# RMS norms of an encoder trunk: sums and factors by 32x32 block turns instead of row products

## The chip, the cores and the metric

The kernel runs on one core of a Trainium2 chip. A core has TensorE (PE in the profile: matrix products, with its weight loads listed apart as PEld), VectorE (DVE), ScalarE (ACT), GpSimd (POOL) and SyncE (SP, which here only issues transfers). PE writes to PSUM, which the kernel divides into eight banks of 128 x 512 float32; the other data live in SBUF, 128 partitions wide. The metric is the device time of one execution in microseconds (us); the figure for a kernel is the median of its runs.

## The reference

Two layers of a bidirectional encoder trunk over 512 tokens of width 1024, all float32:

```python
h = rms_norm(x, attn_norm_g[l])
proj = h @ w_in[l]      # latents, rotary key, GQA q/k/v, pool channels, 3 gates
... three branches: latent attention, grouped-query attention, pooling
merged = gates[0]*(o_mla @ w_b0) + gates[1]*(o_gqa @ w_b1) + gates[2]*(o_pool @ w_b2)
x = x + merged @ w_out[l]
hf = rms_norm(x, ffn_norm_g[l])
u = depthwise_conv(hf @ ffn_w_up[l], ...)          # 2 x 2816 columns, width 3
x = x + (silu(u_gate) * u_val) @ ffn_w_down[l]

def rms_norm(x, g):
    return x * rsqrt(mean(x*x, axis=-1) + 1e-6) * g
```

There are thus four norms over the 1024 features: one ahead of attention and one ahead of the feed-forward part, in each of two layers. Smaller norms (latents, heads) exist too; of those the change touches one step of the grouped-query heads' norm.

## The kernel before, in words

The residual stream lies in SBUF feature-major: `XM` is eight chunks (kc) of 128 features (partitions) by 512 tokens. Every product is made of three products of 32-bit "fp32r" operands, each number split into a high and a low half: `HH` and `HL` are the halves of x times the gain g (without the token's factor), `wh` and `wl` those of a piece of the weights. Weights stream in by SP; ACT makes `wh`, and POOL (or DVE) makes `wl = raw - wh`, three pieces ahead of use (`LA = 3`). A block of output is 8 chunks x 3 products = 24 products of 128x512. So the token's factor rsqrt(mean + eps) is not needed before a product; it is multiplied in when a PSUM bank is emptied. It is needed in two layouts:

- by token on partitions (`rt`, used through `rtok(b)` for the four blocks b of 128 tokens), for results that come token-major: the latents, GQA q, k and v;
- by token along the free axis, the same on all partitions (`rbc`, 128 x 512), for results that come feature-major: pool channels, gates, the up-projection.

A norm runs so. As each chunk of x is finished, ACT squares it and POOL (DVE in the first norm) adds the squares into `sq`, 128 x 512, element by element, so `sq` still has 128 partial sums for each token, one on each partition. `norm_finish` then takes the sums over partitions: four float32 products with two columns of ones, one for each block of 128 tokens, into the one bank "S". DVE makes mean plus eps, POOL raises it to the power -0.5 (128 x 8), which is `rt`. For the other layout DVE splits `rt` into halves `rth` and `rtl` and multiplies each into the identity (`dgh`, `dgl`, 128 x 512); `norm_rows` multiplies ones with these two diagonals on PE and ACT copies the result to `rbc`.

What sets the order of the work: each engine executes its own queue in order. The queues are written by a planner inside the program, the class `Clock`: every instruction is booked with an estimated cost on its engine, `chain` issues the next step of a sequence when the step before is finished by these books, `need` moves the planner's time on until a key is done, and `has` asks whether a key is done by now. So the place of an instruction in its queue follows from booked costs; on the chip it then waits on semaphores for its data. PE products advance the planner's time.

The places that matter here:

- `layer(l, ...)`: first the latent projection, token-major, into the banks acc, acc, ST, ST (`tok_major(latb, 384)`); then four pooling groups, feature-major, into AV, AV, mi, S (`feat_major`, which yields after each of the eight chunks); then GQA q (`gqb`), k and v.
- The latents are emptied by ACT with the factor (`lat_evac`), then normalized; the chain waits for `rt`. The tables of rotary factors are made on POOL after `rt`, too, in the first layer.
- Norm of the first layer's attention: `norm_finish` is called after the sixth chunk of the first pooling group, `norm_rows` after the second group. Second layer: `norm_finish` right after the latent projection, `norm_rows` after the first group.
- Feed-forward norms: `norm_finish` after the first block of 24 products of the up-projection, `norm_rows` after the second. The up-projection has 44 blocks of 24 products, in three tags of two banks each.
- `gq_mean`: DVE turns the sums of squares of the 8 heads x 4 blocks (`ssr`, 128 x 32) into mean plus eps, one tensor_scalar; Newton steps on DVE follow. Around it in DVE's queue stand the steps that empty the pooling product's banks (`opl`), which later gate products need.
- The start: DVE fills a few constants, PE runs nine idle products of ones (`idle`), SP loads x, the first weights, then the constants `C`.

Of the kernel before, what the change touches and what calls it, by code (L numbers as in the profile page):

```python
# [10 lines left out]
F32 = mybir.dt.float32  # L11
F32R = mybir.dt.float32r
# [6 lines left out]
P = 128  # L19
T = 512  # L20
# [35 lines left out]
PRM_MQ = PRM_B + 2 * FC  # L56
NPRM = PRM_MQ + 2

C_ID, C_CG, C_SG, C_CM, C_SM, C_EDGE = 0, 128, 384, 640, 768, 896
NCST = C_EDGE + 64  # L60


def _order(br):
# [59 lines left out]
class Clock:  # L123
# [129 lines left out]
def trunk(ctx: ExitStack, tc: tile.TileContext, x, w, prm, gb, cst, out):  # L253
# [48 lines left out]
    def f(ap):  # L302
        return ap.bitcast(F32)
# [55 lines left out]
    def mm(o, lhsT, rhs, start, stop):  # L359
        PE.matmul(o, lhsT=lhsT, rhs=rhs, start=start, stop=stop)  # L360
        ck.to(ck.now + max(0.107, rhs.shape[-1] / 2370.0))
# [15 lines left out]
    idr = cp.tile([P, P], F32R, tag="idr", name="idr")  # L377
# [3 lines left out]
    mhalf = cp.tile([P, 1], F32, tag="mhalf", name="mhalf")  # L381

    unit = cp.tile([P, P], F32R, tag="unit", name="unit")

# [68 lines left out]
            return [guess, *[lambda to=to: newton(to) for to in (y, y, a)], lambda: done(*key)]  # L453
        return [go, lambda: done(*key)]

    def norm_finish(gen, sq, out):

        need(*[("sq", gen, kc) for kc in range(KC)])
        s2 = ps("S")
        for b in range(4):  # L460
            mm(s2[:, 2 * b:2 * b + 2], sq[:, b * P:b * P + P], f(ones[:, :2]), True, True)
        rt = out["rt"] = small("rt", [P, 8])
        rh, rl = small("rth", [P, 8], F32R), small("rtl", [P, 8], F32R)
        dg = out["dg"] = slot("dgh", F32R), slot("dgl", F32R)

        def mean():
            V.tensor_scalar(rt, s2[:, :8], 1.0 / D, EPS, ALU.mult, ALU.add)
            free("S")

        def diag(n):  # L470
            r = f((rh, rl)[n]).rearrange("p (b t) -> p b t", t=2)[:, :, 0:1]
            V.tensor_tensor(dg[n][:, :T].rearrange("p (b q) -> p b q", b=4), bc(ident[:, None, :], [P, 4, P]),
                            bc(r, [P, 4, P]), ALU.mult)

        chain(mean, *rsqrt_steps(rt, 8, ("rt", gen)), lambda: V.tensor_copy(rh, rt),
              lambda: V.tensor_tensor(rl, rt, f(rh), ALU.subtract), lambda: diag(0), lambda: diag(1),
              lambda: done("dg", gen), after=0.4)

    def norm_rows(gen, out, tag):

        need(("dg", gen))
        r = ps(tag)
        for n in range(2):
            mm(r, ones, out["dg"][n][:, :T], n == 0, n == 1)
        rbc = out["rbc"] = slot("rbc")
        chain(lambda: (A.activation(rbc[:, :T], r, AF.Copy), free(tag), done("rbc", gen)))

    def copy(out, in_, psum=True, bias=C_BIAS):

        n = 1  # L490
        for d in out.shape[1:]:
            n *= d
        act = max(ck.now, ck.free.get("ACT", 0.0)) + 0.09 + 0.00084 * n
        dve = max(ck.now, ck.free.get("DVE", 0.0)) + 0.07 + (0.00105 if psum else 0.00053) * n
        if dve + bias < act:
            V.tensor_copy(out, in_, psum)
        else:
            A.activation(out, in_, AF.Copy)

    def bc(ap, shape):  # L500
        return ap.to_broadcast(shape)
# [26 lines left out]
    def layer(l, sq, xsrc):  # L528
# [68 lines left out]
        nrm = {}  # L597
        ltags = ("acc", "acc", "ST", "ST")
        latb = [ps(t) for t in ltags]
        tok_major(latb, 384)  # L600
        if l:
            norm_finish(G1, sq, nrm)

        def rtok(b):
            return nrm["rt"][:, 2 * b:2 * b + 1]

        mx = [slot("mx") for _ in range(4)]
        ssc = small("ssc", [P, 4, 2])
# [23 lines left out]
        if l:  # L632
            latents()


        mixed = {}
# [44 lines left out]
        for g in range(4):  # L681
            acc = ps(ptags[g])
            for n, _ in enumerate(feat_major(acc, G1)):
                if l == 0 and g == 0 and n == 5:
                    norm_finish(G1, sq, nrm)
                    latents()
# [74 lines left out]
            chain(add, lambda: done("gqr", l, b), after=ck.fin - ck.now)  # L761

        def gq_mean():
            V.tensor_scalar(ssr[:, 0:32], ssr[:, 0:32], 1.0 / 64, EPS, ALU.mult, ALU.add)

        def gq_token():
            s_ = ssr[:, 0:32].rearrange("p (b h) -> p b h", b=4)
            V.tensor_tensor(s_, s_, bc(nrm["rt"].rearrange("p (b t) -> p b t", t=2)[:, :, 0:1], [P, 4, 8]), ALU.mult)

        def gq_norm(b):  # L770
            o = gqo[b][:, :T].rearrange("p (h f) -> p h f", f=64)
# [712 lines left out]
            chain(*steps)  # L1484

        n = 0
        for c in range(FC):
            for part in range(2):
                tag = tags[n % 3]
                n += 1  # L1490
                acc = ps(tag)
                run(feat_major(acc, G2))
                if n == 1:
                    norm_finish(G2, sq, fin)
                if n == 2:
                    norm_rows(G2, fin, "mi")
                up_evac(c, part, acc, tag)

        last = l == L - 1
# [49 lines left out]
    sq = slot("sq")  # L1549
    nc.scalar.dma_start(prms[0][:, :PRM_W0], prm[0][:, :PRM_W0])  # L1550
    warm = small("warm", [P, 1], bufs=1)
    V.memset(mhalf, -0.5)
    V.memset(warm, 0.0)
    A.activation(warm, warm, AF.Exp)
    V.memset(f(ones), 1.0)
    G.memset(f(unit), 0.0)
    G.memset(f(unit[:, 0:1]), 1.0)
    idle = ps("mi")
    for _ in range(9):
        PE.matmul(idle, lhsT=ones, rhs=ones[:, None, :].to_broadcast([P, 4, P]), start=True, stop=True)  # L1560
    free("mi")
    for kc in range(KC):
# [125 lines left out]
def _constants():  # L1688
    cg, sg = _tables(64)
    cm, sm = _tables(32)  # L1690
    t = np.arange(T)
    edge = []
    for w in WINDOWS:
        cnt = np.clip(t + w - w // 2, 0, T) - np.clip(t - w // 2, 0, T)
        r = w / cnt
        edge += [r[:8], r[-8:]]
    edge = np.broadcast_to(np.concatenate(edge).astype(np.float32), (P, 64))
    return np.concatenate([np.eye(P, dtype=np.float32), cg, sg, cm, sm, edge], axis=1)


# [22 lines left out]
```

## Time and profile before

| | us |
|---|---|
| median of 3 runs | 1612.09 (1611.22 to 1614.61) |
| the profiled execution's own time | 1611.31 |
| its span, first to last instruction | 1609.5 |
| PE busy | 1600.2 |
| POOL busy | 1002.6 |
| DVE busy | 950.0 |
| ACT busy | 793.8 |

The profile is of one execution. Its page gives the busy time of each engine, the span in 40 slices, the queues of transfers, the chain of work that ended last, and groups of instructions. Further views of the same trace are used: the waits (who waited for whom), groups by line or by tile (count, then least, median and most ns), and the timeline (start in us, length in us, engine, line, operation, out<-in, shape, count; a bracket gives the idle time just before it and what ended it). Most instructions are issued by small helpers, so L360 is any product, L221 any tensor_tensor, L233 any tensor_scalar, L225 any scalar_tensor_tensor; the tile names tell them apart. Lengths of PE's products overlap: what one costs is the distance between starts.

### The profile page before, as it was taken

To read this page: it belongs to the slowest core of one execution; us is meant where nothing else is said; L and a number is where in the kernel's file an instruction comes from. 1 tells how busy PE (TensorE), PEld (TensorE's weight loads), DVE (VectorE), ACT (ScalarE), POOL (GpSimd) and SP (SyncE) were. 2 spreads that over 40 slices of the span, in tenths; PEclk is the share of its full clock that TensorE was granted. 3 is DMA by queue.
4 is the path that set the end of the run, shared out by engine and by line. 5 is a ranking of instruction groups with operands and counts; after the bars stand their busy time and mean duration, and the time that the engine had idled before them with its cause. 6 is when DMAs were issued, how large, how long until landed. Compare 5 with 4: busy or idle time off the path is not lost.

```text
span 1609.5 us, 20515 instructions
## 1 busy us (share of the span) xinstructions
PE 1600.2 (99%) x7131; PEld 1313.1 (82%) x7131; DVE 950.0 (59%) x1533; ACT 793.8 (49%) x1430; POOL 1002.6 (62%) x889
## 2 busy tenths in 40 slices
PE   9999999999999999999999999999999999999999
PEld 8888888788888888888888888888888888888888
DVE  6878867765276666611047788678552766666000
ACT  6457757663444444433244577576533444444221
POOL 3864985854666665654568549868547566665542
PEclk9999999999999999999999999999999999999999
DMA  5432234414323323233335222343242222222331
GB/s 198 130 104 67 76 115 114 117 59 145 104 87 97 92 92 94 93 115 111 105 105 131 92 76 70 104 139 96 79 144 92 92 92 92 93 93 103 118 112 46
DMA packets 85928, 164.37 MB, mean 102 GB/s; under 512 B 25024, under 2 KB 47040, under 8 KB 85824
## 3 DMA queue, kind: packets, MB, share of 16 engines
q1 hardware_dynamic: 80928, 162.85, 32.5%
q8 instruction: 56, 0.92, 0.2%
q10 hardware_dynamic: 4896, 0.21, 0.2%
q14 instruction: 48, 0.39, 0.1%
HBM read 149.33 MB, written 13.63 MB: 101 GB/s over the span
## 4 chain that ended last, share of the span: by engine, by line
PE 93%; DVE 2%; issue 1%; POOL 1%; ACT 1%; DMA 1%; SPq 0%; ACTq 0%; POOLq 0%
PE ps_acc L360 41%; PE ps_AV L360 22%; PE ps_ST L360 22%; PE ps_S L360 3%; PE ps_mi L360 3%; DVE XM L221 1%; DMA tf<-dtq 1%; POOL wl L221 0%; DVE mgl L221 0%; DVE gt L225 0%; ACT mgh L214 0%; DMA qa<-nm 0%; DMA dtq<-tr 0%; PE ps_mi L1560 0%; POOL gqr L221 0%
## 5 line engine op out<-in xcount | busy, mean ns | idle before, releaser
L221 POOL TENSOR_TENSOR wl<-raw,wh 128x512 fp32r<-128x512 f32 (+2 forms) x502 | 659.9, 1325 | 464.8 <-ACT wh L214 377.5
L214 ACT ACTIVATE wh<-raw 128x512 fp32r<-128x512 f32 (+1 forms) x521 | 308.3, 607 | 124.0 <-PE ps_ST L360 40.7
L225 DVE SCALAR_TENSOR_TENSOR a<-u,prm,a 128x512 f32<-128x512 f32 x176 | 239.0, 1359 | 79.4 <-ACT a L214 74.1
L360 PE MATMUL ps_acc<-HH,wh 128*128 128x512 f32 x592 | 234.9, 397 | 0.5 <-DVE gt L221 0.5
L360 PE MATMUL ps_acc<-HL,wh 128*128 128x512 f32 x592 | 234.1, 395 | 0.0
L360 PE MATMUL ps_acc<-HH,wl 128*128 128x512 f32 x592 | 233.4, 394 | 0.0
L360 PEld LDWEIGHTS ps_acc<-HH,wl 128*128 128x128 f32 x592 | 111.2, 188 | 27.3
L360 PEld LDWEIGHTS ps_acc<-HH,wh 128*128 128x128 f32 x592 | 111.5, 188 | 26.1 <-issue 1.1
L360 PEld LDWEIGHTS ps_acc<-HL,wh 128*128 128x128 f32 x592 | 111.3, 188 | 25.4
L360 PE MATMUL ps_AV<-HH,wh 128*128 128x512 f32 x288 | 114.3, 397 | 1.6 <-DVE y L233 1.6
L360 PE MATMUL ps_AV<-HL,wh 128*128 128x512 f32 x288 | 113.8, 395 | 0.0
L360 PE MATMUL ps_AV<-HH,wl 128*128 128x512 f32 x288 | 113.5, 394 | 0.0
L229 DVE TENSOR_REDUCE nm<-ps_S 128x1 fp32r<-128x512 f32 x128 | 87.6, 685 | 39.9 <-PE ps_S L360 38.3
L221 POOL TENSOR_TENSOR al<-a,ah 128x512 fp32r<-128x512 f32 x44 | 58.1, 1320 | 84.9 <-ACT ah L214 56.5
L360 PE MATMUL ps_ST<-HH,wh 128*128 128x512 f32 x240 | 95.3, 397 | 0.0
L360 PE MATMUL ps_ST<-HL,wh 128*128 128x512 f32 x240 | 95.0, 396 | 0.0
L360 PE MATMUL ps_ST<-HH,wl 128*128 128x512 f32 x240 | 94.3, 393 | 0.0
L214 ACT ACTIVATE a<-u,prm 128x512 f32<-128x512 f32 x88 | 71.8, 816 | 33.3 <-DVE u L221 33.3
L214 ACT ACTIVATE ah<-a 128x512 fp32r<-128x512 f32 x44 | 27.8, 631 | 116.1 <-DVE u L249 110.7
L214 ACT ACTIVATE a<-a 128x512 f32<-128x512 f32 x44 | 27.8, 632 | 113.0 <-DVE u L249 113.0
L214 ACT ACTIVATE HH<-XM,prm 128x512 fp32r<-128x512 f32 x32 | 23.1, 722 | 106.2 <-DVE XM L221 55.1
L214 ACT ACTIVATE ps_ST<-ps_ST 128x512 f32<-128x512 f32 x86 | 49.9, 581 | 41.3 <-PE ps_ST L360 38.9
(385 smaller groups left out, 3751.0 us busy)
## 6 DMA issues: line engine op xcount, KB each, us to landing
raw<-w SPq DMA_DIRECT2D x228, 512.0 KB, 3.5
raw<-w SPq DMA_DIRECT2D x13, 384.0 KB, 3.1
XM<-x SPq DMA_DIRECT2D x16, 256.0 KB, 3.9
dtq<-tr SPq DMA_DIRECT2D x16, 192.0 KB, 3.3
dtk<-tr SPq DMA_DIRECT2D x16, 192.0 KB, 4.2
tf<-dtq SPq DMA_DIRECT2D x48, 64.0 KB, 2.5
tf<-dtk SPq DMA_DIRECT2D x48, 64.0 KB, 2.7
raw<-w SPq DMA_DIRECT2D x6, 448.0 KB, 3.4
```

Of the source, the lines that this page charges most:

```text
L214: return self.eng.activation(out, in_, func, **k)
L221: return self.eng.tensor_tensor(out, *a)
L225: return self.eng.scalar_tensor_tensor(out, *a)
L229: return self.eng.tensor_reduce(out, in_, *a, **k)
L360: PE.matmul(o, lhsT=lhsT, rhs=rhs, start=start, stop=stop)
```

## The change

Each norm's sums go another way. `norm_begin`, called at the start of the stage, turns `sq` on DVE in 32x32 blocks as soon as the last square is added; a sum over groups of 32 elements then leaves `part`, 128 x 16: for each of the 16 groups of 32 tokens, the sums over each quarter of the partitions, tokens now on partitions within each quarter. `norm_finish` multiplies this on PE with one constant 128 x 128 matrix `C_GRP`, which adds the four quarters and puts the result on all of them. DVE makes mean plus eps, POOL the power, now on 128 x 16. From these 16 columns both layouts come on DVE: `tokens` picks the column of the partition's quarter with the constant `C_SEL` and adds over four, giving `rt` (128 x 4); `rows` turns the 16 columns, each repeated 32 times, in 32x32 blocks, giving `rbc`. `norm_rows`, the diagonals, the halves and ACT's copy are gone. `norm_finish` is now called after every chunk of the pooling groups and of the up-projection's blocks; it issues the product when the planner's books have `part` ready, or at a forced place. `latents()` is set up before the pooling groups in both layers.

The other edits: `gq_mean` becomes a scalar_tensor_tensor with a broadcast tile of eps; the tile `idr` and its copy go; at the start `ones` is filled first, there are eight idle products instead of nine, and the constants are 1104 columns wide instead of 960.

```diff
-    def norm_finish(gen, sq, out):
-        need(*[("sq", gen, kc) for kc in range(KC)])
+    def norm_begin(gen, sq):
+        t, part = slot("sqT"), small("prt", [P, 16])
+        parts[gen] = part
+        chain(([("sq", gen, kc) for kc in range(KC)], lambda: V.transpose(t[:, :T], sq[:, :T])),
+              lambda: V.tensor_reduce(part, t[:, :T].rearrange("p (j r) -> p j r", r=32), AX.X, ALU.add),
+              lambda: done("prt", gen), after=0.0)
+
+    def norm_finish(gen, out, force=False):
+        if gen not in parts or not (force or ck.has(("prt", gen))):
+            return
+        need(("prt", gen))
         s2 = ps("S")
-        for b in range(4):
-            mm(s2[:, 2 * b:2 * b + 2], sq[:, b * P:b * P + P], f(ones[:, :2]), True, True)
...
+        mm(s2[:, :16], C[:, C_GRP:C_GRP + P], parts.pop(gen), True, True)
+        a, a4 = small("fac", [P, 16]), small("fac4", [P, 16])
+        rt, rbc = out["rt"], out["rbc"] = small("rt", [P, 4]), slot("rbc")
         def mean():
-            V.tensor_scalar(rt, s2[:, :8], 1.0 / D, EPS, ALU.mult, ALU.add)
+            V.tensor_scalar(a, s2[:, :16], 1.0 / D, EPS, ALU.mult, ALU.add)
             free("S")
...
-        chain(mean, *rsqrt_steps(rt, 8, ("rt", gen)), lambda: V.tensor_copy(rh, rt),
-              lambda: V.tensor_tensor(rl, rt, f(rh), ALU.subtract), lambda: diag(0), lambda: diag(1),
-              lambda: done("dg", gen), after=0.4)
-
-    def norm_rows(gen, out, tag):
...
+        def tokens():
+            V.tensor_tensor(a4, a, C[:, C_SEL:C_SEL + 16], ALU.mult)
+            V.tensor_reduce(rt, a4.rearrange("p (b g) -> p b g", g=4), AX.X, ALU.add)
+            done("rt", gen)
+        def rows():
+            V.transpose(rbc[:, :T].rearrange("p (j r) -> p j r", r=32), bc(a.unsqueeze(2), [P, 16, 32]))
+            done("rbc", gen)
+        chain(mean, lambda: G.tensor_tensor(a, a, bc(mhalf, [P, 16]), ALU.pow), tokens, rows, after=0.3)
...
+        norm_begin(G1, sq)
         tok_major(latb, 384)
-        if l:
-            norm_finish(G1, sq, nrm)
...
             for n, _ in enumerate(feat_major(acc, G1)):
-                if l == 0 and g == 0 and n == 5:
-                    norm_finish(G1, sq, nrm)
-                    latents()
-            if g == (l == 0):
-                norm_rows(G1, nrm, "acc")
+                norm_finish(G1, nrm, g == 1 and n == 6)
...
-            V.tensor_scalar(ssr[:, 0:32], ssr[:, 0:32], 1.0 / 64, EPS, ALU.mult, ALU.add)
+            V.scalar_tensor_tensor(ssr[:, 0:32], ssr[:, 0:32], 1.0 / 64, bc(eps, [P, 32]), ALU.mult, ALU.add)
...
+        norm_begin(G2, sq)
...
-                run(feat_major(acc, G2))
-                if n == 1:
-                    norm_finish(G2, sq, fin)
-                if n == 2:
-                    norm_rows(G2, fin, "mi")
+                for i, _ in enumerate(feat_major(acc, G2)):
+                    norm_finish(G2, fin, n == 3 and i == 6)
...
-    V.memset(mhalf, -0.5)
+    V.memset(f(ones), 1.0)
     V.memset(warm, 0.0)
     A.activation(warm, warm, AF.Exp)
-    V.memset(f(ones), 1.0)
+    V.memset(mhalf, -0.5)
+    V.memset(eps, EPS)
...
-    for _ in range(9):
+    for _ in range(8):
...
-    at(30.0, lambda: V.tensor_copy(idr, ident))
```

More of the change, by code (lines that the diff above doesn't have):

```diff
@@ L57 @@
 NPRM = PRM_MQ + 2
-C_ID, C_CG, C_SG, C_CM, C_SM, C_EDGE = 0, 128, 384, 640, 768, 896
-NCST = C_EDGE + 64
+C_ID, C_CG, C_SG, C_CM, C_SM, C_EDGE, C_GRP, C_SEL = 0, 128, 384, 640, 768, 896, 960, 1088
+NCST = C_SEL + 16
 def _order(br):
@@ L376, in trunk @@
     C = cp.tile([P, NCST], F32, tag="C", name="C")
-    idr = cp.tile([P, P], F32R, tag="idr", name="idr")
     xsp = dp.tile([KC, P, T], F32, tag="xsp", name="xsp")
@@ L381, in trunk @@
     mhalf = cp.tile([P, 1], F32, tag="mhalf", name="mhalf")
+    eps = cp.tile([P, 1], F32, tag="eps", name="eps")
     unit = cp.tile([P, P], F32R, tag="unit", name="unit")
@@ L454, in rsqrt_steps @@
         return [go, lambda: done(*key)]
-    def norm_finish(gen, sq, out):
-        need(*[("sq", gen, kc) for kc in range(KC)])
-        s2 = ps("S")
-        for b in range(4):
-            mm(s2[:, 2 * b:2 * b + 2], sq[:, b * P:b * P + P], f(ones[:, :2]), True, True)
-        rt = out["rt"] = small("rt", [P, 8])
-        rh, rl = small("rth", [P, 8], F32R), small("rtl", [P, 8], F32R)
-        dg = out["dg"] = slot("dgh", F32R), slot("dgl", F32R)
+    def norm_begin(gen, sq):
[4 more added lines that the diff above has]
+              lambda: done("prt", gen), after=0.0)
@@ L479, in norm_rows @@
-    def norm_rows(gen, out, tag):
[L481 to L486, printed above, removed]
+        def tokens():
+            V.tensor_tensor(a4, a, C[:, C_SEL:C_SEL + 16], ALU.mult)
+            V.tensor_reduce(rt, a4.rearrange("p (b g) -> p b g", g=4), AX.X, ALU.add)
+            done("rt", gen)
@@ L498, in copy @@
             A.activation(out, in_, AF.Copy)
+    parts = {}
     def bc(ap, shape):
@@ L630, in latents @@
                   *rsqrt_steps(ssc.rearrange("p a b -> p (a b)"), 8, ("ssc", l)), lat_norm)
-        if l:
-            latents()
+        latents()
         mixed = {}
@@ L1697, in _constants @@
     edge = np.broadcast_to(np.concatenate(edge).astype(np.float32), (P, 64))
-    return np.concatenate([np.eye(P, dtype=np.float32), cg, sg, cm, sm, edge], axis=1)
+    p = np.arange(P)
+    group = (p[:, None] % 32 == p[None, :] % 32).astype(np.float32)
+    sel = (p[:, None] // 32 == np.arange(16)[None, :] % 4).astype(np.float32)
+    return np.concatenate([np.eye(P, dtype=np.float32), cg, sg, cm, sm, edge, group, sel], axis=1)
 def kernel(**inputs):
```

9 lines of the change are left out of this document (2 added, 7 removed).

## The prediction

> **What bounds the kernel now.** I read the page first: part 1 (busy time of each engine), the slices, and part 4 (the chain that ended last).
>
> ```profile
> PE 1600.2 (99%) x7131; PEld 1313.1 (82%) x7131; DVE 950.0 (59%) x1533; ACT 793.8 (49%) x1430; POOL 1002.6 (62%) x889
> PEclk9999999999999999999999999999999999999999
> PE 93%; DVE 2%; issue 1%; POOL 1%; ACT 1%; DMA 1%; SPq 0%; ACTq 0%; POOLq 0%
> ```
>
> TensorE (PE) works nearly without a break, at full granted clock in every slice, and 93% of the chain is PE. So a product that disappears from PE shortens the run by its own spacing, a stall of PE that disappears by its length, and work on other engines counts only where PE ends up waiting for it. The view of waits, PE alone, gives the stalls (us in total, times, longest):
>
> ```profile
> PE ps_AV L360 <- DVE y L233: 1.6, 1, 1.6
> PE ps_mi L1560 <- DVE ones L249: 1.1, 1, 1.1
> PE ps_mi L360 <- DMA qa<-nm: 0.7, 1, 0.7
> ```
>
> Beside the 1.1 us before PE's first instruction and the 1.6 us stall, nothing is above 0.7 us.
>
> **Term 1, products removed.** The timeline of PE around the second layer's feed-forward norm:
>
> ```profile
> 1241.07 0.40 PE L360 MATMUL ps_acc<-HH,wl 128*128 128x512 f32 x1
> 1241.31 0.95 PE L360 MATMUL ps_S<-ones,sq 128*128 128x2 f32 x8
> 1242.12 0.48 PE L360 MATMUL ps_ST<-HH,wh 128*128 128x512 f32 x1
> 1242.43 0.39 PE L360 MATMUL ps_ST<-HL,wh 128*128 128x512 f32 x1
> 1242.66 0.40 PE L360 MATMUL ps_ST<-HH,wl 128*128 128x512 f32 x1
> ...
> 1247.57 0.39 PE L360 MATMUL ps_ST<-HH,wl 128*128 128x512 f32 x1
> 1247.80 0.39 PE L360 MATMUL ps_mi<-dgh,ones 128*128 128x512 f32 x1
> 1248.02 0.46 PE L360 MATMUL ps_mi<-dgl,ones 128*128 128x512 f32 x1
> 1248.32 0.42 PE L360 MATMUL ps_AV<-HH,wh 128*128 128x512 f32 x1
> ```
>
> Ordinary products start 0.23 us apart (1242.43 to 1242.66); the 0.4 us beside each is its length in a pipeline, not its price. From 1241.07 to 1242.43 would be two steps, 0.46; it is 1.36. So the four float32 sums, eight records, cost 0.90 us. From 1247.57 to 1248.32 would be one step; it is 0.75, so the two row products cost 0.52. A norm pays 1.42, and there are four (the groups of these tiles, all with counts over the run; columns after the colon are least, median and most ns):
>
> ```profile
> L360 PE MATMUL ps_S<-ones,sq x32: 166/251/251, 26.4 to 1242.0; 128*128 128x2 f32 x32
> L360 PE MATMUL ps_acc<-dgh,ones x2: 392/395/398, 34.3 to 828.7; 128*128 128x512 f32 x2
> L360 PE MATMUL ps_mi<-dgh,ones x2: 389/393/397, 447.5 to 1247.8; 128*128 128x512 f32 x2
> ```
>
> The two row products of each attention norm I count at the plain spacing, 0.46. Sum: 4 x 0.90 + 2 x 0.52 + 2 x 0.46 = 5.6 us; taken **-5.6**.
>
> **Term 2, the product added.** One float32 product of a 128x128 constant with 16 columns at each norm. The nearest row is the one just used: four such products with 2 columns cost 0.90, so 0.23 for one, in two records. Fourteen more columns at 0.23 us per 512 columns are 0.01. From below: half of it, 0.11, if the neighbours hide the weight loads; from above 0.46, one record more at each end. I take 0.25: **+1.0** (0.4 to 1.8).
>
> **Term 3, what the product waits for.** The partial sums need a turn of sq and a sum over 32 elements on DVE, behind the last addition. Rows of the first norm (timeline) and the two durations (groups):
>
> ```profile
> 20.72 4.95 DVE L221 TENSOR_TENSOR sq<-sq,sqt 128x512 f32<-128x512 f32 x4
> 26.43 0.95 PE L360 MATMUL ps_S<-ones,sq 128*128 128x2 f32 x8
> 27.41 0.17 DVE L233 TENSOR_SCALAR rt<-ps_S 128x8 f32<-128x8 f32 x1 [1.75 <-PE ps_S L360]
> L245 DVE STREAM_TRANSPOSE osum<-oinv 128x512 f32<-128x512 f32 x16 | 11.3, 708 | 1.8 <-POOL oraw L221 0.9 <-ACT oinv L214 0.2
> L229 DVE TENSOR_REDUCE ssr<-gqs 128x8 f32<-128x512 f32 x8 | 5.2, 673 | 0.0
> ```
>
> Sums end at 25.67; turn 0.71 and sum 0.67 end at 27.05, and DVE is free for them (idle 1.75). PE reaches the place at 26.43 if the product goes where the four go now, after the sixth step of the first pooling group: it waits about 0.6. Does it go there? The code issues it at the first step at which the planner's own clock (a count of booked costs, no time of the chip) has the sums ready. The books add 0.61 + 0.13 + 0.61 + 0.15 for turn and sum to a last addition at 23.2, giving 24.7, and reach the sixth step at 24.8: same place, by a hair. One step later the wait is gone (0.7 us a step); one earlier it is 1.3. **+0.6** (0 to 1.3).
>
> The feed-forward norms have no such wait: there the planner, which until now stops at the sums, goes on and issues the product some four steps (2.8 us) into the second column block. The four sums at 1241.31 already had the finished additions, so turn and sum, 1.4 us, end by 1242.7; PE gets there near 1244. In the second layer's attention norm the product follows the whole latent projection, near 823, and this is its last addition:
>
> ```profile
> 809.20 1.29 POOL L221 TENSOR_TENSOR sq<-sq,sqt 128x512 f32<-128x512 f32 x1
> ```
>
> Both cost nothing.
>
> **Term 4, the other edit.** The mean of the squares, 128x32, and what stood around it (DVE, POOL and PE timelines; second layer first, then the first layer's same step):
>
> ```profile
> 876.72 8.30 DVE L233 TENSOR_SCALAR ssr<-ssr 128x32 f32<-128x32 f32 x1
> 884.94 0.74 DVE L225 SCALAR_TENSOR_TENSOR opl<-ps_AV,prm,oph 128x512 fp32r<-128x512 f32 x1
> 879.19 5.79 POOL L221 TENSOR_TENSOR wl<-raw,wh 128x288 fp32r<-128x288 f32 x5
> 883.98 0.29 PE L360 MATMUL ps_ST<-wh,HL 128*128 128x288 f32 x1
> 885.82 0.47 PE L360 MATMUL ps_AV<-HH,wh 128*128 128x512 f32 x1 [1.56 <-DVE y L233]
> ...
> 76.66 0.22 DVE L233 TENSOR_SCALAR ssr<-ssr 128x32 f32<-128x32 f32 x1
> 80.18 1.21 DVE L225 SCALAR_TENSOR_TENSOR y<-yt,y 128x32 f32<-128x32 f32 x1
> ```
>
> The same instruction took 0.22 once and 8.30 once, ending when POOL's unbroken run (to 884.98) ended. Queued behind it is opl, which empties the bank that PE's first gate product needs: PE starts at 885.82 instead of about 884.1. The new form is a SCALAR_TENSOR_TENSOR of the same size; small ones with POOL running take up to 1.21, one POOL instruction. Then opl is done by 879 and the stall goes. Next late is the second gate bank, needed 24 steps or 5.6 us after the first; the first layer has that order and no ps_AV stall. **-1.7** (0 to -1.7).
>
> A rule of the Trainium skill speaks against this. SBUF — State Buffer, "Who interferes with whom", says that a DVE instruction with two SBUF inputs also contends with a GpSimd one that reads SBUF, and that the lock is held for a whole instruction. By that rule the new form (eps is a second SBUF input) stays exposed, and the sum would be -4.1 instead of -5.8. The 8.30 fits no lock for one POOL instruction, so the trace goes beyond the rule; the 1.21 row agrees with it.
>
> **Term 5, the start.** One of nine idle products goes and ones is filled first.
>
> ```profile
> 1.11 4.21 PE L1560 MATMUL ps_mi<-ones 128*128 128x512 f32 x9 [1.11 <-DVE ones L249]
> 3.71 0.72 ACT L214 ACTIVATE HH<-XM,prm 128x512 fp32r<-128x512 f32 x1 [1.03 <-DMA prm<-prm]
> 4.69 0.76 PEld L360 LDWEIGHTS ps_acc<-wh,HH 128*128 128x128 f32 x2
> ```
>
> The first real load at 4.69 waits for HH (done 4.43), so little is won: **-0.1** (-0.4 to +0.3). The constants grow by 15%; first used near 27 us, they are covered. The copy idr on DVE goes, unseen by PE.
>
> **What moves off PE's path, at nothing.** DVE loses a cast, a subtraction and two 128x512 products, and gains a turn, two sums, a small product and the final turn; ACT loses the copy of rbc. POOL's power takes 16 columns for 8:
>
> ```profile
> L221 POOL TENSOR_TENSOR rt<-rt,mhalf x4: 1644/1652/1654, 27.7 to 1242.5; 128x8 f32<-128x8 f32 x4
> 40.61 2.59 POOL L221 TENSOR_TENSOR wl<-raw,wh 128x512 fp32r<-128x512 f32 x2
> 46.00 0.40 PE L360 MATMUL ps_AV<-wh,HH 128*128 128x512 f32 x1
> 450.96 3.05 POOL L221 TENSOR_TENSOR wl<-raw,wh 128x512 fp32r<-128x512 f32 x2 [4.59 <-PE ps_AV L360]
> 832.10 1.68 POOL L221 TENSOR_TENSOR wl<-raw,wh 128x512 fp32r<-128x512 f32 x1 [2.37 <-issue]
> 840.51 5.60 PE ps_S L360 x24
> ```
>
> It lies between 1.65 and 3.3. Behind it on POOL stand weight halves (wl); behind the factor on ACT stand the latent evacuations or the convolution steps, and behind those the other halves (wh). With the two tiny DVE sums (0.17 to 1.2 each) the factor comes 0.6 to 3.7 us later in the attention norms. The cover: the first wl of the pair at 40.61 ends at 41.9 and is used at 46.0, 4.1 us; the one that starts at 450.96 ends near 452.4 and is used in the fourth column block near 456.4, 4.0 us. In the second layer's attention norm the half ready at 833.8 is used at 840.5, 6.7 us. So late by 3.7 still costs nothing; beyond 4 us PE pays one for one. The rows of the factor themselves come earlier in the first layer (no row products to await).
>
> **Sum.** -5.6 + 1.0 + 0.6 - 1.7 - 0.1 = -5.8 us. The profiled execution took 1611.31 (span 1609.5), giving 1605.5; it lies 0.8 below the median 1612.09. Against the median I forecast **1606.3**.
>
> **Rivals.** *The DVE stall stays* (small steps of either form stuck behind POOL): term 4 is nothing, 1608.0. For: 128x32 steps that wait for POOL at all; against: the SCALAR_TENSOR_TENSOR row above, also beside POOL's run, took 1.21. *New stalls take the gain:* the planner's order shifts by under a microsecond at each norm, and waits like the 0.7 us one multiply in attention; with 3 to 6 us of them, 1609 to 1612. Against: both layers' attention now has under 2 us of stalls. *Slower:* a tiny DVE step of the new factor is held as long as the mean was, 8.3 us, at every norm. It decides from 4 us on: PE then pays 8.3 - 4.1 in the first layer, 8.3 - 4.0 in both feed-forwards, and some 1.6 in the second attention norm (cover 6.7), 14.4 in all: 1620.7. Against: the step of the TENSOR_SCALAR form among them reads PSUM and took 0.17 at all four norms.
>
> **Chances.** Forecast 0.55 (own range 1604.8 to 1608.2); stall stays 0.2; new stalls 0.15; slower 0.07; better still by the remaining small stalls 0.03. About 0.2%, 3.2 us, is what a measurement here can tell from no change: faster is below 1608.9. All but little of the first two cases and the last lies there, 0.70 with a part taken off for unseen shifts; within 0.21; slower 0.09. The range for 8 in 10, out to most of the new-stall case: 1604.3 to 1611.3.
>
> **What would show it.** Right: two ps_S records from the constant at each norm, no row products; a PE wait of about 0.6 at 27 us; no 8.3 us mean at 877 and no ps_AV stall at 885; feed-forward blocks back to back. Wrong: PE waiting for wl or wh within 20 us behind a norm (POOL's power or a held tiny step), a new long DVE step beside POOL's run, or PE waits in attention above 2 us together.

## The result, and the profile after

| | before | after |
|---|---|---|
| median, us | 1611.22 (1609.09 to 1614.61, 5 runs) | 1590.24 (1589.31 to 1593.7, 5 runs) |
| the profiled execution | 1611.31 | 1593.7 |
| its span | 1609.5 | 1591.8 |

The ratio is 0.987 (95% interval 0.9853 to 0.9888): 21 us faster, where 5.8 were forecast and the range ended at 1604.3. From part 1, the slices and part 4 of the page of the changed kernel:

```profile
PE 1576.7 (99%) x7098; PEld 1307.8 (82%) x7098; DVE 959.3 (60%) x1536; ACT 788.3 (50%) x1426; POOL 1022.3 (64%) x890
PEclk9999999999999999999999999999999999999999
PE 89%; DVE 3%; POOL 2%; issue 2%; ACT 2%; DMA 2%; SPq 1%; POOLq 0%; ACTq 0%
```

PE is still the bound, at the same full clock, but its busy time fell by 23.5 us with only 33 records fewer; what is outside PE's busy time rose from 9.3 to 15.1. So far more went than the products removed, and waits were added. The waits of PE in the changed kernel (us in total, times, longest):

```profile
PE ps_acc L360 <- DVE vm L221: 2.0, 2, 1.3
PE ps_AV L360 <- DVE y L233: 1.7, 1, 1.7
PE ps_ST L360 <- ACT oph L214: 1.6, 2, 0.8
PE ps_acc L360 <- POOL wl L221: 1.4, 2, 0.7
PE ps_S L360 <- DVE prt L229: 1.0, 1, 1.0
PE ps_acc L360 <- ACT wh L214: 0.9, 1, 0.9
```

Where the 23.5 us went is seen in the chain, at blocks that the change does not touch (start, length, engine, tile, line, products in the piece). Up-projection and down-projection of the first layer, before:

```profile
453.75 5.60 PE ps_acc L360 x24
...
698.63 15.30 PE ps_ST L360 x66
```

and after:

```profile
455.25 5.44 PE ps_acc L360 x24
...
693.58 15.32 PE ps_ST L360 x66
```

A block of 24 products took 5.60 us and takes 5.44, 233 and 227 ns from start to start. Each of the 88 blocks of the up-projection gives 0.16: 14.1 us, in work the diff does not name. The chains of 66 products of the down-projection did not move. The first kind has HH or HL as an operand, the second has `ah` and `al`, which lie in slots, the kernel's general buffers.

Summed by stage, from the starts of the products in the traces (us; kernels of the experiments below are in the same table; "out + up" is the attention's output projection, eight blocks and 44.7 us before, and then the up-projection):

| | before | after | after, again (e12) | e1 | e2 | e11 | e9 | e8 |
|---|---|---|---|---|---|---|---|---|
| attention 1 | 389.6 | 392.7 | 390.3 | 388.9 | 394.6 | 387.0 | 387.2 | 388.3 |
| out + up 1 | 292.5 | 284.3 | 284.4 | 285.7 | 291.4 | 285.2 | 283.8 | 284.4 |
| down 1 | 122.4 | 122.5 | 122.5 | 122.4 | 122.6 | 119.7 | 119.7 | 122.3 |
| attention 2 | 385.3 | 380.5 | 381.2 | 386.3 | 382.8 | 379.6 | 377.5 | 380.6 |
| out + up 2 | 292.7 | 284.5 | 284.5 | 285.8 | 291.5 | 285.1 | 283.8 | 284.4 |
| down 2 | 122.3 | 122.6 | 122.6 | 122.3 | 122.6 | 120.4 | 120.4 | 122.1 |

The two rows with the up-projections give 16.4 of the 17.7 us between the two profiled spans: 14.1 by the spacing and, as terms 1 and 2 would have it, 2.3 by the products that the norms save there. Attention gains 4.8 in the second layer and loses 3.1 in the first.

### The profile page after: what moved, and what is told of

It reads as the page before. It is cut to its first block, busy times and chain, and to the rows that moved or that the text cites. A ratio compares the mean times of both kernels' runs of the same rounds, so it can differ in the third digit from the quotient of the medians.

```text
span 1591.8 us, 20451 instructions
## 1 busy us (share of the span) xinstructions
PE 1576.7 (99%) x7098; PEld 1307.8 (82%) x7098; DVE 959.3 (60%) x1536; ACT 788.3 (50%) x1426; POOL 1022.3 (64%) x890
## 4 chain that ended last, share of the span: by engine, by line
PE 89%; DVE 3%; POOL 2%; issue 2%; ACT 2%; DMA 2%; SPq 1%; POOLq 0%; ACTq 0%
PE ps_acc L360 41%; PE ps_AV L360 21%; PE ps_ST L360 21%; PE ps_S L360 3%; PE ps_mi L360 3%; POOL wl L221 1%; SPq L707 1%; DMA tf<-dtq 1%; POOL win L221 1%; DVE ssr L225 1%; ACT wh L214 0%; DMA tf<-dl 0%; DVE sq L221 0%; DVE XM L221 0%; DMA XM<-x 0%
## 5 line engine op out<-in xcount | busy, mean ns | idle before, releaser
L221 POOL TENSOR_TENSOR wl<-raw,wh 128x512 fp32r<-128x512 f32 (+2 forms) x503 | 674.4, 1353 | 422.3 <-ACT wh L214 326.5
L214 ACT ACTIVATE wh<-raw 128x512 fp32r<-128x512 f32 (+1 forms) x521 | 308.6, 607 | 129.9 <-PE ps_ST L360 44.7
L225 DVE SCALAR_TENSOR_TENSOR a<-u,prm,a 128x512 f32<-128x512 f32 x176 | 244.5, 1391 | 86.4 <-ACT a L214 83.5
```

The lines of the kernel that those rows point to most:

```text
L214: return self.eng.activation(out, in_, func, **k)
L221: return self.eng.tensor_tensor(out, *a)
L225: return self.eng.scalar_tensor_tensor(out, *a)
```

## The experiments

### What made untouched products faster: addresses or order

The diff moves data in SBUF, which the prediction did not look at. In the compiled programs C grows by 576 bytes (144 columns), `idr` (512) goes, `eps` (32 with its padding) comes: all that is allocated behind C, the weight halves and the slots among it, starts 96 bytes later. HH starts at byte 17536 of each partition in both; HL 16384 behind it, `wl` 12288 behind `wh`, their buffers 2048 apart. `wh` starts at 94240 before, which is 416 past a multiple of 512 from HH, and at 94336 after, an exact multiple. My theory was this layout; the rival was order: the new queues leave less beside the products. Four kernels change nothing but the width of one tile, and so addresses.

```diff
-    C = cp.tile([P, NCST], F32, tag="C", name="C")
+    C = cp.tile([P, NCST + n], F32, tag="C", name="C")[:, :NCST]
```

n = 24 in before (e1), 488 in after (e2), 8 in before (e3), 8 in after (e4).

> The kernel before with the constants' tile C made 24 columns (96 bytes) wider and nothing else; every tile allocated behind C, the weight halves wh and wl and the slots among them, then begins 96 bytes later, where it begins in the changed kernel. HH and HL do not move. Layout theory (a product that takes one operand from HH or HL and one from wh or wl runs at a spacing set by their addresses): a block of 24 up-projection products takes 5.44 us as in the changed kernel, not 5.60; 88 blocks x 0.16 is 14.1 us, with the pooling groups and gates some 16, so about 1595 us. Order theory (the products run faster because the changed kernel issues them in another order or has less DVE and ACT work beside them): instructions and order are those of before, so blocks stay at 5.60 and the time at 1611.

> The changed kernel with C made 488 columns (1952 bytes) wider: wh and wl then begin exactly 2048 bytes behind their places in the kernel before, so at the same place in every unit of 2048 bytes or less. Layout theory: blocks of 24 go back to 5.60 us and the time rises by some 16 us to about 1606, which would be the forecast of 1606.3 for the norms alone. Order theory: blocks stay at 5.44, time 1590.

> The kernel before with 32 bytes more in C: wh and wl then begin on a multiple of 64 bytes as in the changed kernel, but 64 bytes short of a multiple of 512 away from HH (the changed kernel: an exact multiple; before: 96 short). Alignment theory (64 bytes by themselves decide): blocks of 24 take 5.44, about 1595 us. Distance theory (what counts is how far wh lies from HH within 512 bytes or so): not 5.44; 5.5 to 5.6, 1603 to 1611. Order theory: 1611.

> The changed kernel with 32 bytes more in C: wh and wl begin 32 bytes past a multiple of 64, and 32 past a multiple of 512 away from HH. Alignment theory: blocks of 24 at 5.60, about 1606 us. Distance theory: near the fast distance but not on it, somewhere in 5.44 to 5.60, 1590 to 1606. Order theory: 1590.

| | wh from HH, past a multiple of 512 | wh past a multiple of 64 | block of 24, us | time, us | ratio to before (95%) |
|---|---|---|---|---|---|
| before | 416 | 32 | 5.60 | 1609.62 | |
| e1: before + 96 | 0 | 0 | 5.44 | 1595.98 | 0.9917 (0.9895 to 0.9939) |
| e2: after + 1952 | 416 | 32 | 5.60 | 1609.87 | 0.9999 (0.9988 to 1.0009) |
| e3: before + 32 | 448 | 0 | 5.49 in layer 1, 5.60 in layer 2 | 1603.22 | 0.9955 (0.994 to 0.9971) |
| e4: after + 32 | 32 | 32 | 5.60 | 1609.73 | 0.9998 (0.9989 to 1.0008) |

The chain of e1, the kernel before with 96 bytes of nothing:

```profile
452.82 5.44 PE ps_acc L360 x24
...
691.12 15.30 PE ps_ST L360 x66
```

and of e2, the changed kernel with its operands back at the old places:

```profile
457.55 5.60 PE ps_acc L360 x24
```

Order is out: e1 issues the instructions of before in the order of before, and its blocks take 5.44. And e2 gives the verdict on the rest of the change at the old addresses: without the shift of 96 bytes it makes no measurable difference, where the layout theory with the forecast for the norms expected about 1606. In e3 the 64-byte multiple gave only part, and of the two up-projections only in one, so it is not alignment alone. e4 alone would fit alignment as well, and lies above the 1606 at which the span expected for distance ended. Whether it is the distance between the operands, two more kernels say. e5 moves everything alike, by a wider tile in front of HH; e6 moves `wh` by 64 with n = 16 in after.

```diff
-    XM = cp.tile([P, KC, T], F32, tag="XM", name="XM")
+    XM = cp.tile([P, KC * T + 8], F32, tag="XM", name="XM")[:, :KC * T].rearrange("p (k t) -> p k t", k=KC)
```

> The changed kernel with 32 bytes put ahead of HH (the tile XM in front of it is 8 columns wider): HH, HL, wh, wl and the slots all move by the same 32 bytes. All of them now begin 32 bytes past a multiple of 64, and wh stays an exact multiple of 512 away from HH. Distance theory: blocks of 24 stay at 5.44 us, time 1590. Alignment theory (each address by itself): 5.60 as with wh alone moved by 32, about 1609.

> The changed kernel with 64 bytes more in C, behind HH and HL and ahead of wh: wh stays on a multiple of 64, 64 past a multiple of 512 away from HH (the kernel before with 32 bytes more had 64 short of one and took 5.49 to 5.56 a block). Distance theory: not 5.44; near 5.5, so some 1595 to 1600 us. Alignment theory (64 bytes, or 32 bytes and the sum of small things): 5.44 and 1590.

e5: 1592.6 us, ratio 0.9886 (0.9863 to 0.991); e6: 1608.6, 0.9987 (0.9974 to 1.0). Chain of e5, then of e6:

```profile
453.65 5.44 PE ps_acc L360 x24
```

```profile
453.55 5.60 PE ps_acc L360 x24
```

With both operands 32 bytes off a multiple of 64 but a multiple of 512 apart the blocks keep 5.44; with both on multiples of 64 but 64 apart they lose it. The distance decides, not the address. e6 was expected near 5.5 like e3 and took all of 5.60.

Two things were open: which distances are short, and why e3 had two spacings at the same addresses. e13 and e14 are the changed kernel with n = 64 and 32, e15 is e3 again.

> The changed kernel with 256 bytes more in C: wh lies 256 past a multiple of 512 from HH. If only multiples of 512 are short: blocks of 24 at 5.60, about 1609 us. If multiples of 256 do: 5.44, 1590. The slots, in the traces so far, have products with the weights 256 away and the moving operands at the same place: 230.9 ns on average over 118 of them, which would be 5.54 and some 1602.

> The changed kernel with 128 bytes more in C: wh lies 128 past a multiple of 512 from HH. Multiples of 512 alone: 5.60, about 1609 us; multiples of 128: 5.44, 1590. Products of the slots at that distance: 231.2 ns over 70, which would be 5.55 and some 1603.

> The kernel before with 32 bytes more once again. In its first trace the blocks of the up-projection took 5.49 us in the first layer and 5.60 in the second, at the same addresses. If addresses alone set the spacing of each block, the same split comes again; if the products fall into one of two rhythms by what went on when the stage began, it can come out otherwise: 5.60 in the first layer, or 5.49 in both, and a time between 1597 and 1609.

e13 took 1592.97 us (two runs), ratio 0.9899 (0.987 to 0.9928), e14 1607.94, 0.9989 (0.9978 to 1.0001), e15 1601.69, 0.9953 (0.994 to 0.9967). Chains of e13, of e14, then of e3 and of e15, up-projections of both layers:

```profile
451.29 5.44 PE ps_acc L360 x24
...
1301.19 5.44 PE ps_AV L360 x24
```

```profile
456.01 5.57 PE ps_acc L360 x24
```

```profile
464.75 5.49 PE ps_AV L360 x24
...
1301.56 5.60 PE ps_ST L360 x24
```

```profile
457.72 5.49 PE ps_ST L360 x24
...
1301.43 5.49 PE ps_ST L360 x24
```

With the weights 256 past a multiple of 512 from the moving operands the blocks are as short as at a multiple; at 128 past they are not. And 64 short of a multiple is not one spacing but two, each kept through a whole up-projection: which one it falls into differs between executions of one program. So the addresses set what is possible, and at that distance something in the execution chooses. What that is was not tried. At the other distances no trace shows a second spacing in the up-projections.

### A second product stream at the same distance: the slots

If distance is the rule, it must show inside one trace too (this was looked at ahead of e13, so by multiples of 512): slots lie 2112 bytes apart, so the products of the down-projection have many distances, in steps of 64 bytes. Grouped by whether the next weights lie a multiple of 512 from the operand that streams, and whether the next moving operand does (addresses from the compiled program, spacing from the trace):

```
changed kernel, down-projection      products  ns from start to start
both multiples of 512 away                 52  228.5
weights only                              127  232.2
moving operand only                        82  233.0
neither                                   729  232.0
```

Only where both hold is the spacing clearly short here. But the trace of before, grouped in the same way, has 16 products with both, and they are not short: 231.8 ns, against 231.3 for its 774 with neither. Single products among others prove little; a whole stream of them is the test. e9 puts all of them there: slots of 512 columns, and five wide ones for the three kinds of tile that need 514 to 528.

```diff
-    sp = ctx.enter_context(tc.tile_pool(name="sp", bufs=NSLOT))
+    sp = ctx.enter_context(tc.tile_pool(name="sp", bufs=46))
+    wp = ctx.enter_context(tc.tile_pool(name="wp", bufs=5))
...
-        t = sp.tile([P, SLOT], dt, tag="s", name=f"{name}_{uid[0]}")
+        wide = name in ("pp", "win", "u")
+        t = (wp if wide else sp).tile([P, SLOT if wide else T], dt, tag="s", name=f"{name}_{uid[0]}")
```

e11 gives the kernel before the same addresses (n = 24 and these pools); e12 is the changed kernel once more beside them.

> The changed kernel with the slots in two pools: 46 of 512 columns (2048 bytes apart) for all tiles that need no more, and 5 of 528 columns for the windows of the pooling and the convolution input u. Every product operand of the down, out and gate projections then lies a multiple of 512 bytes from wh, wl and from each other; with slots 2112 bytes apart nearly none did. Phase theory (a product starts 227 ns after the last if both moving operands and the weights lie a multiple of 512 apart, 231 to 234 if not): a down-projection chain of 66 products takes 66 x 0.2267, 14.96 us, in place of 15.31; 16 chains give 5 us, the products of the attention up to some 5 more, so 1581 to 1585. Rival (the spacing there has another limit): 15.31 and 1590. Against both: with only 5 wide slots the pooling or the convolution may wait; each microsecond of such waits comes on top.

> The kernel before with the same addresses: C 96 bytes wider and the slots in the same two pools. Against the changed kernel with these slots it gives what the norms and the new mean are worth with addresses equal. By the terms of the prediction's sum for the products (-5.6 + 0.9 + 1.0 as measured, -0.4 for the idle product) 4 us slower than that one; with the new stalls of the first layer (some 3 us) taken off, 1 us slower; by the pair at the addresses of before (1609.6 and 1609.9) no slower at all.

> The changed kernel once more, beside the other three on the same chip, as their common base: 1590.

e9: 1579.4 us, ratio to before 0.9817 (0.9801 to 0.9834), better than expected; e11: 1583.53, 0.9839 (0.9824 to 0.9853); e12: 1591.07, 0.9886 (0.9871 to 0.99); before: 1609.11. The chain of e9 (two lines were added, so L362):

```profile
454.62 5.44 PE ps_ST L362 x24
...
702.13 14.96 PE ps_AV L362 x66
```

14.96 was the number expected, and all 990 products of the table above now have both distances and start 226.7 ns apart. e9 sets both distances at once, so it does not tell them apart. The two stages down lose 5.0 us, attention 6.8 (e9 against e12). The five wide slots cost no wait that shows.

The pair e11 and e9 prices the change itself with addresses equal and fast: 1583.53 to 1579.4, 4.1 us, the first of the three values expected. The four runs of each do not overlap (1583.16 to 1583.97, 1578.8 to 1581.54). In the stage table: up-projections -1.4 and -1.3, attention 2 -2.1, attention 1 +0.2.

### What became of the held step and of the late factor

e7 puts the mean of the squares back into its old form.

```diff
-            V.scalar_tensor_tensor(ssr[:, 0:32], ssr[:, 0:32], 1.0 / 64, bc(eps, [P, 32]), ALU.mult, ALU.add)
+            V.tensor_scalar(ssr[:, 0:32], ssr[:, 0:32], 1.0 / 64, EPS, ALU.mult, ALU.add)
```

> The changed kernel, at its own addresses, with the mean of the squares back in its old form (one TENSOR_SCALAR, no eps input). In the changed kernel the new form is held 8.3 us in the first layer and 2.6 in the second, in the kernel before the old form 0.22 and 8.3. Theory (the hold goes with POOL's unbroken run at that place and not with the form): held near 8 us in the first layer again, PE waits 1.7 us for y at 88, time within 2 us of 1590. Rival (the form matters): the old form is not held in the first layer, the wait for y goes, 1588 to 1589; or it is held in both, 1592.

It took 1589.71 us, ratio 0.9871 (0.9846 to 0.9896). The step in e7 (timeline of DVE):

```profile
80.02 1.28 DVE L233 TENSOR_SCALAR ssr<-ssr 128x32 f32<-128x32 f32 x1
...
868.94 1.28 DVE L233 TENSOR_SCALAR ssr<-ssr 128x32 f32<-128x32 f32 x1
```

By itself that speaks for the rival: the old form was not held in either layer. But the new form does both. In the profiled execution of the changed kernel (DVE, then POOL):

```profile
78.73 8.34 DVE L225 SCALAR_TENSOR_TENSOR ssr<-ssr,eps 128x32 f32<-128x32 f32 x1
...
871.46 2.57 DVE L225 SCALAR_TENSOR_TENSOR ssr<-ssr,eps 128x32 f32<-128x32 f32 x1
...
78.69 2.58 POOL L221 TENSOR_TENSOR gqr<-gqr,rp 128x512 f32<-128x512 f32 x2
81.17 5.85 POOL L221 TENSOR_TENSOR wl<-raw,wh 128x288 fp32r<-128x288 f32 x5
```

and in e12, the same program executed again:

```profile
79.05 1.31 DVE L225 SCALAR_TENSOR_TENSOR ssr<-ssr,eps 128x32 f32<-128x32 f32 x1
...
79.03 2.53 POOL L221 TENSOR_TENSOR gqr<-gqr,rp 128x512 f32<-128x512 f32 x2
81.53 5.82 POOL L221 TENSOR_TENSOR wl<-raw,wh 128x288 fp32r<-128x288 f32 x5
```

In the one the step came 0.04 us behind the start of POOL's run and got through only when that run ended, seven instructions later; in the other it came 0.02 behind and got through after one. Over the 17 traces at hand the step was held over 8 us in 9 of its 34 executions, 2 of 12 in the old form and 7 of 22 in the new. It goes one way or the other from execution to execution of one program, and both forms are found on both sides; these few cases cannot tell whether the form changes the odds. It costs 1.5 to 1.7 us when it loses: in all nine PE waits that long for the first gate bank, and in none of the other 25. The wait for y in the first list above is one of them, and e12 has none.

The late factor: in the first layer the factor starts ACT at 32.69 after, at 29.34 before (the changed kernel's row is shown below; this is ACT before).

```profile
29.34 0.58 ACT L214 ACTIVATE mx<-ps_acc,rt 128x384 f32<-128x384 f32 x1 [6.28 <-POOL rt L221]
```

e8 brings the token column forward.

```diff
-            done("rt", gen)
...
-        chain(mean, lambda: G.tensor_tensor(a, a, bc(mhalf, [P, 16]), ALU.pow), tokens, rows, after=0.3)
+        chain(mean, tokens, lambda: G.tensor_tensor(rt, rt, bc(mhalf, [P, 4]), ALU.pow), lambda: done("rt", gen),
+              lambda: G.tensor_tensor(a, a, bc(mhalf, [P, 16]), ALU.pow), rows, after=0.3)
```

> The changed kernel with the factor's two uses in another order: the token column is picked from the mean first (128x16 product and sum on DVE) and raised to the power on 4 columns on POOL; the power of all 16 columns, for the rows alone, comes behind it. The token factor should be ready 3 us earlier than in the changed kernel (one short power instead of 2.9 us and a DVE step that waits for it). Theory (the stalls of PE between 64 and 88 us, some 4 us in the first layer, come from latents that start 3.4 us later than before): stalls shrink to under 2 us, time 1586 to 1588. Rival (they come from another order of the planner, not from the late factor): 1590, stalls as they are.

It took 1588.72 us, ratio 0.9861 (0.9839 to 0.9884), between what the theory and the rival expected. Timelines of e8 (POOL, ACT, SP's queue, PE):

```profile
28.67 1.01 POOL L221 TENSOR_TENSOR rt<-rt,mhalf 128x4 f32<-128x4 f32 x1 [4.63 <-DVE gcol L221]
29.72 0.58 ACT L214 ACTIVATE mx<-ps_acc,rt 128x384 f32<-128x384 f32 x1 [6.48 <-POOL rt L221]
58.69 0.33 SPq L314 DMA_DIRECT2D raw<-w  x1
59.19 6.27 SPq L707 DMA_DIRECT2D tf<-dl  x12
69.43 0.40 PE L360 MATMUL ps_acc<-wh,HH 128*128 128x288 f32 x1 [0.31 <-ACT wh L214]
70.54 0.40 PE L360 MATMUL ps_acc<-wl,HH 128*128 128x288 f32 x1 [0.71 <-POOL wl L221]
78.30 0.48 PE L360 MATMUL ps_ST<-mxh,wh 128*128 128x512 f32 x1 [0.81 <-ACT oph L214]
```

The same in the changed kernel:

```profile
28.26 2.90 POOL L221 TENSOR_TENSOR fac<-fac,mhalf 128x16 f32<-128x16 f32 x1 [4.21 <-DVE fac L233]
32.69 0.58 ACT L214 ACTIVATE mx<-ps_acc,rt 128x384 f32<-128x384 f32 x1 [9.52 <-DVE rt L229]
57.55 1.74 POOL L221 TENSOR_TENSOR wl<-raw,wh 128x512 fp32r<-128x512 f32 x1
59.32 0.33 SPq L314 DMA_DIRECT2D raw<-w  x1
59.82 6.35 SPq L707 DMA_DIRECT2D tf<-dl  x12
70.09 0.40 PE L360 MATMUL ps_acc<-wh,HH 128*128 128x288 f32 x1 [0.88 <-ACT wh L214]
```

And before (DVE, POOL, SP's queue):

```profile
53.24 1.31 DVE L221 TENSOR_TENSOR wl<-raw,wh 128x512 fp32r<-128x512 f32 x1
53.96 1.74 POOL L221 TENSOR_TENSOR wl<-raw,wh 128x512 fp32r<-128x512 f32 x1
55.73 0.33 SPq L314 DMA_DIRECT2D raw<-w  x1
57.90 6.17 SPq L710 DMA_DIRECT2D tf<-dl  x12
```

The factor is 3.0 us earlier, as meant, and attention 1 is 2.0 shorter than in e12, where the mean was not held either. Little of this came by the way that the theory named. The wait for `wh` shrank from 0.73 to 0.31; those for `wl` and `oph` stayed. Of the rest, 0.55 is the wait for `prt`, which stands ahead of the edited step (1.43 in e12, 0.88 here, 0.95 in the first execution of the changed kernel), and 0.66 a wait for `vm` near 245 us, which was 0.61 in before and 1.09 in e1, two kernels with the same instructions.

The latents come back by a transfer (`tf`) that starts 0.6 us earlier, not 3. It did not wait for the latents: the transfers that carry them out (`dl`) had all landed by 57.27 in the changed kernel and by 56.04 in e8, before at 57.84. It stands in SP's queue right behind a weight transfer, and that one fills a buffer again whose two halves `wl` have to be made first: by 55.70 before, by 59.29 in the changed kernel, by 58.66 in e8, each time within 0.05 us of its start. Before, POOL made one of the two and DVE the other (53.96 and 53.24); in the planner's new order POOL makes both, one behind the other, the second from 57.55 on (from 57.36 in e8). So the transfer is late by the new order, and the late factor is seen in the 0.4 us at `wh`. Whether it has a part in POOL's lateness too was not separated.

e10 joins e8's edit with e9's.

> The two edits together: slots 2048 bytes apart, and the token factor picked and raised ahead of the rows. If they add: the slots' gain (5 to 9 us by the phase theory) and the 1.5 us (times) to 5 us (spans) of the earlier token factor, 1578 to 1583. If the waits of the first layer come from the planner and not from the factor: as the slots alone.

1577.97 us, ratio 0.9802 (0.9788 to 0.9817), against 0.9817 for the slots alone. The two intervals overlap; the pair e8 and e12 points the same way, so about 1.5 us is likely, not proven. It is the fastest kernel of the study, 31 us below before.

## Why the prediction was wrong

The direction came out as forecast, but by luck: at the addresses of before the same change makes no difference (e2), and what made it faster stood nowhere in the forecast. The size was far off: 1606.3 forecast, 1590.2 measured, out of a range that was built from waits alone.

**The step that failed** is the opening part's "a product that disappears from PE shortens the run by its own spacing", used with the spacing of all others, 0.23 us, as fixed. The change moves that spacing. The addresses alone are worth 13.6 us in one direction (before to e1) and 18.8 in the other (e2 to e12, from two sets of runs in which before took 1609.62 and 1609.11); the forecast had nothing for them. The edits that did it stand in the diff. Term 5 looked at two of them for their time alone and put it at nothing (constants 15% larger, a tile gone); the small tile added it does not name. No rival named the addresses either. The trace of before showed 5.60 for every block of the up-projection, with no shorter block beside it, so the profile alone gave no sign; that tiles change their sizes stood in the diff.

The Trainium skill states in SBUF — State Buffer, "Who interferes with whom", that PE reads its moving operand and its weights through two independent ports and never waits on anyone. Here the spacing of the same products went from 233 to 227 ns as the two operands' distance went from 416 past a multiple of 512 bytes to a multiple, e1 against before. The measurement decides: the two are not independent in their addresses. What in the chip does it, no run here shows.

**Term 1 and 2** held where they can be seen alone. The up-projections with addresses equal and slow (e2 against before) lose 1.1 and 1.2, with addresses fast (e9 against e11) 1.4 and 1.3, for 1.42 removed and 0.25 added. The new product costs 0.23, in the place forecast, twelve products into the second block (timeline of PE, changed kernel):

```profile
446.46 0.39 PE L360 MATMUL ps_ST<-HH,wl 128*128 128x512 f32 x1
446.69 0.29 PE L360 MATMUL ps_S<-prt,C 128*128 128x16 f32 x2
...
447.14 0.40 PE L360 MATMUL ps_ST<-HL,wh 128*128 128x512 f32 x1
```

From 446.46 to 447.14 is 0.68, less two steps of 0.23.

**Term 3** was 0.6 and measured 0.95 (the bracket of the first norm's product):

```profile
27.57 0.39 PE L360 MATMUL ps_S<-prt,C 128*128 128x16 f32 x2 [0.95 <-DVE prt L229]
```

The place was right; the turn began at 26.09, 0.4 us later than summed. Executions of the changed kernel and its variants have 0.5 to 1.4 there.

**Term 4** was wrong: the new form does not keep the step free. Its gain of 1.7 in the second layer was real in the profiled execution, and was paid again in the first. The rival "the DVE stall stays" was right that the new form can be stuck, though what the runs show is now one outcome and now the other. The Trainium skill, in the same section of SBUF — State Buffer, has the lock held for a whole instruction; here seven POOL instructions went by (8.34 us), as the 8.30 in the prediction had already shown, so this trace goes beyond what the page says.

**What was put at nothing.** "Late by 3.7 still costs nothing" held where the prediction looked: the factor was 3.35 late in the first layer, inside the cover named, and the view of waits has none of PE's between 27.57 and 70.09. The cost stands further on, in what the prediction did not follow, the new order on POOL and in SP's queue: the transfer `tf` starts 1.9 us later than before, and PE waits for `wh`, `wl` and `oph` at 70.09, 71.20 and 78.96 (0.88, 0.71 and 0.82), where before has no wait. With slow addresses attention 1 loses 5.0 (e2 against before) where -0.6 was forecast; 1.6 of that is the held step, which e2 has in the first layer and before in the second.

So the sum for the norms at the old addresses came out at no difference (ratio 0.9999), as the rival "new stalls take the gain" has it (1609 to 1612, given 0.15; e2 gave 1609.87). With the fast addresses (e11 to e9, and no step held in either profile) it was 4.1, which is the forecast without term 4. That these two agree is in part luck: attention 1 got 0.2 longer where 0.6 shorter was forecast, and attention 2 2.1 shorter where 1.1 was. Why the same change is worth nothing at one set of addresses and 4.1 us at another stays open.

## What to carry to other kernels

When a change resizes, adds or removes a tile, look at where the others land: with PE as the bound, a shift of 96 bytes was worth three to five times the 4.1 us that the edit gave at equal, fast addresses. Before a kernel's edits are compared, give both the same addresses (a few unused columns do it), or the measurement is of the layout too. And lay out operands of products a multiple of 512 bytes from each other, wherever a buffer is a little wider than it must be: here that gave another 11.7 us (e12 to e9). A distance of 256 past a multiple was as good for the weights against HH and HL (e13); between moving operands it was not tried.

## What the hardware showed that I had not expected

The spacing of two PE products (fp32r, 128x128 weights, 512 columns) depends on the distance in SBUF between the moving operand and the weights: 227 ns at a multiple of 512 bytes and at 256 past one, 232 to 233 at 128 past, 233 at 96 short, 32 past and 64 past, and 229 or 233 at 64 short, from stage to stage. In these runs successive moving operands, HH and HL, lay a multiple of 512 apart. That this second distance counts too is suggested by the slots (232.2 with the weights alone at a multiple, 226.7 when all have both), but was not tried by itself. All of it is seen at full granted clock.

A small DVE step beside an unbroken run of POOL can be held to the end of that run, 8.3 us over seven instructions, or only for one of them, 1.3 us, in two executions of one program.

Faster products gave less than their sum where other engines are near: from before to e1 PE's busy time fell by 17.5 us and the span by 13.4, since the time outside PE's busy time rose by 4.1; attention 2 got 1.0 longer while its blocks on HH and HL got shorter.
